# Who ends an upsampling kernel: GpSimd releases the other engines before the last store has landed, and ends alone

## The chip, the cores and the metric

One core of a Trainium2 chip. The metric is the device time of one execution in microseconds, the median of several; every run is of one core, with a granted clock of 1.0. "Span" is the time from the first to the last instruction of the program itself in a profiled execution; it is shorter than the measured time, and this case is about why.

In the profile, POOL is GpSimd, DVE is VectorE, ACT is ScalarE, PE and PEld are TensorE, and SP is SyncE, which issues the transfers; a "q" behind the name marks an instruction that the engine's sequencer (the part that runs its instruction stream) handles alone. Three such instructions make up the program's closing block: an EVENT_SEMAPHORE waits for semaphores, changes one, or both; a RANGE_CLEAR sets a row of semaphores to zero; a DRAIN stands here between other instructions, and can wait for a semaphore too. "Landing" is the moment of the last store's final semaphore increment.

## The reference

Nearest-neighbour upsampling by 2: each pixel of 16 x 64 images of 64 x 64 floats is written four times.

```python
batch, channels, h, w = (16, 64, 64, 64)
...
for i in range(new_h):
    for j in range(new_w):
        src_i = i // scale_factor
        src_j = j // scale_factor
        result[:, :, i, j] = x[:, :, src_i, src_j].copy()
```

That is 16.78 MB in and 67.11 MB out.

## The kernel before

SP issues five loads and twelve stores; VectorE and ScalarE expand the rows in between. The stores are 4 MB or 8 MB, and the last one is 8 MB:

```python
nc.vector.tensor_copy(out=u[:, :kv], in_=expanded(xp[:, r0 : r0 + kv, :]))
nc.scalar.copy(out=u[:, kv:], in_=expanded(xp[:, r0 + kv : r0 + k, :]))
...
return nc.sync.dma_start(out=dst[:, r0 : r0 + k, :], in_=u)
```

Two hooks rearrange the finished program. One issues the first load before the opening barrier. The other, which is what changes, rearranges the closing block. That block has GpSimd gather all engines and release them, twice; between the two it must wait for all stores and set the semaphores back to zero for the next execution. The kernel before already had GpSimd wait for the stores (a cut of its lines):

```python
d0, gather0, release0, d1, clear, d2, gather1, release1 = mine
landed = mybir.InstDrain(          # waits for all ten semaphores, the last store's too
    name=wait.name, engine=pool, ...
    sync_info=mybir.SyncInfo(on_wait=waits, on_update=[]),
)
others = [i for i in end if i.engine != pool and i is not wait]
blocks[-1].instructions = others + [
    d0, gather0, release0, gather1, d1, landed, clear, d2, release1
]
```

`clear` zeroes the ten semaphores 99 to 108; 99 is the one that the last store raises (and the first load and an earlier store: 3 x 16 = 48). `release1` lets the other four engines end.

## Time and profile before

| | kernel before |
|---|---|
| median of the first three runs | 199.01 us (198.98 to 199.02) |
| span of the profiled run | 197.41 us |
| its measured time | 199.19 us |
| last packet of the last store ends | 196.70 us |
| semaphore 99 complete (the landing) | 197.037 us |
| GpSimd's last instruction ends | 197.326 us |
| last instruction of the program (TensorE) ends | 197.414 us |
| last record of the runtime's barrier, semaphore 2 | 199.319 us |

The lines behind the upper half are in the prediction below. The last row is not on the profile's page; it comes from the trace's records of semaphore updates, which go on after the program. Here they are, for the kernel before, in ns after the landing:

```
semaphore 2:   +612 +646 +851 +895 +919  +1017 +1056 +1090 +1137
resets:        207..255 from +1036, 156.. from +1154, 54.. from +1195, the lowest block ends at +1700
semaphore 2:   +1925 +1959 +1997 +2041 +2065  +2163 +2201 +2235 +2282
```

The nine updates are one pass of a barrier over five engines, which sign it in turn: five updates going up and four coming back. The measured time is 0.13 us less than the time of the very last update (199.19 against 199.319 here).

### The profile page before, as it was taken

Reading aid. Unit: us, or ns where it says so; the run is one execution under the profiler, and the core shown is the slowest. Engines: PE = TensorE matmul, PEld = TensorE weight load, DVE = VectorE, ACT = ScalarE, POOL = GpSimd, SP = SyncE. Lnnn points to the kernel's source line nnn. Section 1 sums busy time; section 2 is a strip of 40 time slices with the busy share of each in tenths; the row PEclk is TensorE's granted clock in tenths of the full one; section 3 lists DMA queues with packets and bytes.
Section 4 is the critical chain, followed back from the end, with each engine's and each line's share of the span. In section 5 each row is a group of like instructions: output and inputs, shape, how many; then the busy total and the mean of one; then the engine's idle time right before and its main releaser. Section 6 shows DMA issues by size and latency. Waiting matters only on the chain.

```text
span 197.4 us, 117 instructions
## 1 busy us (share of the span) xinstructions
DVE 40.2 (20%) x12; ACT 51.3 (26%) x13; POOL 0.2 (0%) x4
## 2 busy tenths in 40 slices
DVE  0045000000505059505050007200810091000000
ACT  2047000000505060606079107400840093000000
POOL 0000000000000000000000000000000000000000
DMA  8999999999999999999999999999999999999994
GB/s 319 425 425 425 438 445 418 411 452 451 432 425 438 425 432 432 425 432 425 425 425 425 425 425 425 478 505 438 438 438 438 438 438 425 425 425 425 425 425 212
DMA packets 2448, 83.89 MB, mean 425 GB/s; under 512 B 272, under 2 KB 272, under 8 KB 400
## 3 DMA queue, kind: packets, MB, share of 16 engines
q1 hardware_dynamic: 2448, 83.89, 98.9%
HBM read 16.78 MB, written 67.11 MB: 425 GB/s over the span
## 4 chain that ended last, share of the span: by engine, by line
DMA 71%; ACT 11%; SPq 1%; issue 0%; ACTq 0%
DMA out_dram<-mem 52%; DMA mem<-in_x_dram 19%; ACT mem L140 11%; SPq L124 0%; SPq L142 0%; ACTq L140 0%
## 5 line engine op out<-in xcount | busy, mean ns | idle before, releaser
L140 ACT COPY mem<-mem 128x3584 f32<-128x3584 f32 (+1 forms) x12 | 50.0, 4174 | 112.5 <-DMA out_dram<-mem 102.1
L139 DVE COPY mem<-mem 128x4608 f32<-128x4608 f32 (+1 forms) x12 | 40.2, 3360 | 123.1 <-DMA out_dram<-mem 110.6
L140 ACT ACT_TABLE_LOAD x1 | 1.3, 1283 | 0.8 <-PEq L178 0.8
L178 POOL MEMSET const-bfloat16-1.0<- 128x1 bf16 x1 | 0.1, 102 | 0.0
L178 POOL MEMSET const-uint8-127<- 128x1 uint8 x1 | 0.1, 101 | 0.0
L178 POOL MEMSET const-float32-0.0<- 128x1 f32 x1 | 0.1, 99 | 0.2 <-issue 0.2
L178 POOL MEMSET const-float32-1.0<- 128x1 f32 x1 | 0.1, 98 | 0.0
## 6 DMA issues: line engine op xcount, KB each, us to landing
out_dram<-mem SPq DMA_DIRECT2D x8, 4096.0 KB, 16.2
mem<-in_x_dram SPq DMA_DIRECT2D x3, 4096.0 KB, 21.4
mem<-in_x_dram SPq DMA_DIRECT2D x1, 3328.0 KB, 38.1
mem<-in_x_dram SPq DMA_DIRECT2D x1, 768.0 KB, 39.4
out_dram<-mem SPq DMA_DIRECT2D x4, 32.4
```

Source lines behind the costliest of these rows:

```text
L139: nc.vector.tensor_copy(out=u[:, :kv], in_=expanded(xp[:, r0 : r0 + kv, :]))
L140: nc.scalar.copy(out=u[:, kv:], in_=expanded(xp[:, r0 + kv : r0 + k, :]))
L178: nc = _bacc.Bacc("TRN2", target_bir_lowering=False, num_devices=1)
```

## The change

The intent is to have as little as possible left to do once the last store has landed. GpSimd releases the others before it waits, clears nine semaphores after the second-last store, and sets the tenth back by the same instruction that waits for it.

```diff
@@
-    waits = sorted(wait.sync_info.on_wait, key=lambda w: w.id != last)
+    waits = list(wait.sync_info.on_wait)
...
+    lo, hi = clear.ant_dict["range_first"], clear.ant_dict["range_last"]
+    clears = []
+    for a, b in ((lo, last), (last + 1, hi + 1)):
+        if a < b:
+            clears.append(nc.gpsimd.sem_clear(range(a, b)).ins)
     landed = mybir.InstDrain(
...
-        sync_info=mybir.SyncInfo(on_wait=waits, on_update=[]),
+        sync_info=mybir.SyncInfo(
+            on_wait=[w for w in waits if w.id != last], on_update=[]
+        ),
     )
+    (w,) = [w for w in waits if w.id == last]
+    final = mybir.InstEventSemaphore(
+        name=clear.name,
+        engine=pool,
...
+            on_wait=[w],
+            on_update=[
+                mybir.SyncUpdate(
...
+                    update_mode="sem-sub-imm",
+                    update_value=w.wait_value,
+                )
+            ],
...
     blocks[-1].instructions = others + [
-        d0, gather0, release0, gather1, d1, landed, clear, d2, release1
+        d0, gather0, release0, gather1, release1, d1, landed, *clears, d2, final
     ]
```

In the built program the range below 99 is empty, so there is one range clear, 100 to 108.

More of the change, by code (lines that the diff above doesn't have):

```diff
@@ L51, in close_on_gpsimd @@
     assert wait.engine == sp and isinstance(wait, mybir.InstDrain)
-    waits = sorted(wait.sync_info.on_wait, key=lambda w: w.id != last)
-    assert waits[0].id == last and len(waits) > 2
+    waits = list(wait.sync_info.on_wait)
+    assert len({w.id for w in waits}) == len(waits) > 2
+    assert all(w.wait_mode == "sem-ge-imm" for w in waits)
     mine = [i for i in end if i.engine == pool]
@@ L67, in close_on_gpsimd @@
     d0, gather0, release0, d1, clear, d2, gather1, release1 = mine
+    lo, hi = clear.ant_dict["range_first"], clear.ant_dict["range_last"]
+    assert lo <= last <= hi and all(lo <= w.id <= hi for w in waits)
+    clears = []
+    for a, b in ((lo, last), (last + 1, hi + 1)):
+        if a < b:
+            clears.append(nc.gpsimd.sem_clear(range(a, b)).ins)
     landed = mybir.InstDrain(
@@ L71, in close_on_gpsimd @@
         debug=wait.debug,
-        sync_info=mybir.SyncInfo(on_wait=waits, on_update=[]),
+        sync_info=mybir.SyncInfo(
[6 more added lines that the diff above has]
+        engine=pool,
+        debug=wait.debug,
+        sync_info=mybir.SyncInfo(
+            on_wait=[w],
+            on_update=[
+                mybir.SyncUpdate(
+                    sync_type=w.sync_type,
+                    id=w.id,
+                    ant_name=w.ant_name,
+                    update_mode="sem-sub-imm",
+                    update_value=w.wait_value,
+                )
+            ],
+        ),
     )
```

## The prediction

> **What bounds the kernel now.** I read the page first (its DMA rows and its chain), then the waits of the store queue, then the instructions of the program's closing block, and last the trace's own records of semaphore updates, because the change lies wholly in that closing block. The page says what the kernel is:
>
> ```profile
> span 197.4 us, 117 instructions
> ...
> DVE 40.2 (20%) x12; ACT 51.3 (26%) x13; POOL 0.2 (0%) x4
> ...
> DMA  8999999999999999999999999999999999999994
> GB/s 319 425 425 425 438 445 418 411 452 451 432 425 438 425 432 432 425 432 425 425 425 425 425 425 425 478 505 438 438 438 438 438 438 425 425 425 425 425 425 212
> ...
> q1 hardware_dynamic: 2448, 83.89, 98.9%
> ...
> DMA 71%; ACT 11%; SPq 1%; issue 0%; ACTq 0%
> ```
>
> The reader is to see that the DMA engines are busy from the first slice to the last: 83.89 MB at 425 GB/s is 197.4 us, the whole span. VectorE and ScalarE are busy a quarter of the time or less. Only the last slice is thin (212 GB/s, digit 4), so that is where a change of the ending can act. A table of stretches narrows it; its columns are the stretch, its length, busy time of VectorE, ScalarE and GpSimd, granted clock, DMA share and GB/s:
>
> ```profile
> 165.50:196.00 30.50, 0.00 (x0) 0.00 (x0) 0.00 (x0) 1.00 0.95 413
> 196.00:196.70 0.70, 0.00 (x0) 0.00 (x0) 0.00 (x0) 1.00 0.01 0
> 196.70:197.40 0.70, 0.00 (x0) 0.00 (x0) 0.00 (x0) 1.00 0.00 0
> ```
>
> After 196.70 us no byte moves. What fills the last 0.7 us is the closing block, listed by engine's queue (count, min/median/max ns, first and last start):
>
> ```profile
> L192 POOLq DRAIN  x2: 34/34/34, 197.1 to 197.2; - x2
> L192 POOLq EVENT_SEMAPHORE_RANGE_CLEAR  x1: 92/92/92, 197.1 to 197.1; - x1
> L192 POOLq EVENT_SEMAPHORE  x1: 17/17/17, 197.3 to 197.3; - x1
> L192 SPq EVENT_SEMAPHORE  x1: 17/17/17, 197.4 to 197.4; - x1
> L192 ACTq EVENT_SEMAPHORE  x1: 17/17/17, 197.4 to 197.4; - x1
> L192 DVEq EVENT_SEMAPHORE  x1: 21/21/21, 197.4 to 197.4; - x1
> L192 PEldq EVENT_SEMAPHORE  x1: 51/51/51, 197.4 to 197.4; - x1
> ```
>
> Line 192 is the end of the program. GpSimd waits for the last store (DRAIN), clears the ten semaphores 99 to 108 with one range clear, drains again, and raises the release semaphore; only then do SP, ScalarE, VectorE and TensorE pass their last wait. With the records to the nanosecond: the last store's final increment of semaphore 99 comes at 197.037; DRAIN 197.061 (34 ns); range clear 197.124 (92 ns); DRAIN 197.246 (34 ns); release 197.309 (17 ns); the four engines' last waits at 197.351, 197.356, 197.362 and 197.363, the last (TensorE, 51 ns) ending at 197.414, which is the span.
>
> The measured time is 199.01 us, 1.6 us more than the span, so something after the program counts too. The semaphore records go on past the span: semaphore 2 is raised nine times at 197.649, .683, .888, .932, .956, 198.054, .093, .127, .174; then semaphores 3 to 255 are written in five blocks of 49 to 51 (207 up from 198.073, 156 up from 198.191, 105 up from 198.228, 54 up from 198.232, the low ones last, to 198.737); then semaphore 2 again nine times, 198.962 to 199.319.
>
> **What the Trainium skill says.** "Runtime: NRT & Kernel Launch", section "Semaphores 0–2 are reserved", has 2 as the sync barrier; its section "The ~15µs preamble/postamble breakdown" puts after the kernel a barrier over all engines, a reset of 51 semaphores by each engine, and another barrier, and calls the barrier a serpentine over five engines of 44 ns a hop, 8 hops. The trace agrees: nine updates, most hops 24 to 47 ns, then the five blocks. "Perfetto Trace Analysis", section "Per-engine timelines" (HWDGE), says that the last descriptor writes the semaphore only after the earlier write is confirmed. The trace shows the last packet ending at 196.70 and the last increment at 197.04, 0.34 us that no ordering of the closing block can shorten. Its summary of sequencer-only instructions says the reported start is the moment the wait is satisfied; 197.037 to 197.061 gives 24 ns for that step here, and 177.690 to 177.713, 23 ns, for an event-semaphore wait on GpSimd.
>
> **The change part by part.** Loads, copies, stores and their waits are untouched: the comparison of the two programs' instruction orders shows the same rows with shifted line numbers on every engine. So all moves after 197.04 us.
>
> Moved early: the second gather and the release. In the kernel before, GpSimd already has everyone's gather at 165.462; now it releases at once, so the four other engines end near 165.6 us instead of 197.4. They then sit in the runtime's barrier for over 31 us, which costs nothing.
>
> Moved early too: the clear. Semaphore 99 is the lowest of the ten, so the range below it is empty and the built program has one range clear, 100 to 108. It runs once the second-last store has landed, that is after 177.71 us, together with d2: 92 and 34 ns, 19 us ahead of the last landing. The waits are nine instead of ten before it, and one instruction of waits is saved there as well, all hidden.
>
> Added at the end: one event-semaphore instruction that waits for 48 on semaphore 99 and subtracts 48. By the 23 ns from increment to start and 17 ns for such an instruction (43 with two waits) it starts at 197.060 and ends at about 197.08.
>
> Sum on GpSimd: it left its program at 197.309 + 0.017 = 197.326; now at 197.078. That is 0.248 us less. The four removed starts spell the same: 63 + 122 + 63 ns from DRAIN to release. On the span as the profile defines it, the last instruction was TensorE's at 197.414, so the span should fall by more, 0.336 us, to 197.08, all else equal.
>
> What of this reaches the measured time depends on who holds up the runtime's barrier. I read its order from the blocks that follow: the low block begins 0.217 us after the ninth update, the 54 block 0.105 after the eighth, 105 after the seventh, 156 after the sixth, and 207 0.117 after the fifth. That is the order TensorE, ScalarE, GpSimd, VectorE, SP, if the blocks are dealt in that order; the same barrier before the program (with its ninth update at -0.002) fits, for SP, first to leave it, issues the first instruction at 0.000. There the third update comes 38 ns after the second; at the end of the program it comes 205 ns after. So the third engine, GpSimd by this reading, is the late one: it needs 197.888 - 197.326 = 0.562 us from its last instruction to its update, whereas TensorE needs 0.235. After that third update everything runs on at fixed hops, 1.431 us to the last update. If GpSimd's 0.562 us stays, its update comes at 197.078 + 0.562 = 197.640 and the whole tail shifts by 0.248 us. The predicted time is 199.01 - 0.25 = 198.76 us, 0.12% less.
>
> **The rivals.** (1) The late third engine is not GpSimd, and its 0.5 us run from the release. Then with all others long waiting, GpSimd would reach the barrier as fast as TensorE does (0.235), its update would come at 197.31, and the gain would be up to 0.57 us: 198.4. Against it: the block order above. (2) The early ends move the barrier's cost elsewhere: GpSimd's 0.562 us may contain a fetch of the code that follows the program, or the subtraction may need more than 17 ns before it can go on. A new 0.1 to 0.2 us would leave 198.9. Against it: GpSimd passed two such wait-and-subtract instructions at 165.135 and 165.462 with 17 ns each, and the next started 78 and 81 ns later. (3) Nothing at all: the four engines, sent into the runtime's code at 165.6 us, fetch or poll while the store queue works, and disturb it; or the measured time is closed by something that does not follow GpSimd. Then 199.0, or a little above. Polling is not seen to hurt: at 165.9 to 196.7 GpSimd's waits stood beside 413 GB/s already. (4) A hang or wrong result if a semaphore were left non-zero: 99 rises to 48 in three transfers of 16 and is taken to 0, and the runtime's block reset includes it anyway.
>
> **The range and the chances.** The spread of the three runs is 0.04 us, so a quarter of a microsecond should be seen, but a different chip or another draw of the last stores' landing can move the whole by 0.1 us or so. Rival 1 draws the low end to 198.5, rivals 2 and 3 the high end to 199.0. Two per cent is 4 us, sixteen times the whole mechanism; and no more than about 0.9 us lies between the last landing and the third update. Faster by over 2% has 0.5%, slower by over 2% (only by disturbance or a slow draw) 0.5%, within 2% 99%.
>
> **What would show it.** Right: GpSimd's last instruction is one event-semaphore of 17 ns or so within 30 ns of the last increment of semaphore 99; the range clear stands near 177.9 us; the other engines' last instructions are near 165.6; the span is about 0.34 us shorter and the measured time only about 0.25; the third barrier update stays 0.56 us behind GpSimd's end, with the first two already made near 165.9. Wrong: a third update that follows GpSimd's end by 0.2 us (rival 1) or by 0.7 (rival 2), or a last landing that has itself moved by more than 0.1 us (rival 3), which would mean that the DMA stream and not the ending decided the difference.

## The result, and the profile after

| | before | changed |
|---|---|---|
| median, 6 runs each | 198.96 us (198.88 to 199.02) | 198.72 us (198.60 to 198.83) |
| ratio, with 95% interval | | 0.9988 (0.9976 to 1.0001) |
| span of the profiled run | 197.414 us | 196.840 us |
| landing | 197.037 us | 196.800 us |
| landing to the last barrier update | 2.282 us | 2.035 us |

Ratios here and below are the mean time of one kernel's fast runs over the mean of the other's of the same rounds, so not quite the ratio of the medians beside them. The medians differ by 0.24 us, and the interval just reaches 1. The timing alone does not establish the difference; the profiles, and the runs below, do.

The page of the changed kernel has the same DMA-filled span:

```profile
span 196.8 us, 117 instructions
...
DMA  8999999999999999999999999999999999999994
...
q1 hardware_dynamic: 2448, 83.89, 99.3%
```

Its closing block, by engine's queue (count, min/median/max ns, first and last start in us). First four of the ten lines of the stretch from 164.9 to 165.6 us:

```profile
L223 SPq EVENT_SEMAPHORE  x2: 17/17/17, 165.0 to 165.3; - x2
L223 ACTq EVENT_SEMAPHORE  x2: 17/17/17, 165.0 to 165.3; - x2
L223 DVEq EVENT_SEMAPHORE  x2: 21/21/21, 165.0 to 165.4; - x2
L223 PEldq EVENT_SEMAPHORE  x2: 51/51/51, 165.0 to 165.4; - x2
```

then the early clear, which has its own line of the source:

```profile
L77 POOLq EVENT_SEMAPHORE_RANGE_CLEAR  x1: 92/92/92, 177.7 to 177.7; - x1
```

and everything that the program still does after 196.5 us:

```profile
L223 POOLq EVENT_SEMAPHORE  x1: 17/17/17, 196.8 to 196.8; - x1
```

The reader is to see that both releases are over at 165.4 us, that the clear lies 19 us ahead of the end, and that of the eight instructions that closed the kernel before (two DRAINs, a range clear, five event-semaphores) a single one is left, of 17 ns. In ns after the landing, the semaphore records of the changed kernel read:

```
semaphore 2:   -31161 -31127  +602 +646 +669  +766 +806 +841 +887
semaphore 2:   +1677 +1711 +1750 +1794 +1817  +1916 +1954 +1988 +2035
```

Two of the five engines now sign the barrier 31 us early. The third, and with it all the rest, is 0.25 us earlier after the landing than before.

The profiled runs differ by more, 199.19 against 198.71. That is 0.247 us from the ending and 0.237 us from an earlier landing, which the change cannot have made: the first store was issued at 39.617 us against 39.864, before any instruction that differs, and from the last store's issue to its landing it took 32.440 us before and 32.444 after. Where a profile's start-to-end times are compared in quarters of a microsecond, they must be anchored at the landing; so I do for all runs.

### The profile page after: what moved, and what is told of

Read it like the earlier page. It is cut to its first block, busy times and chain, and to the rows that moved or that the text cites. A ratio compares the mean times of both kernels' runs of the same rounds, so it can differ in the third digit from the quotient of the medians.

```text
span 196.8 us, 117 instructions
## 1 busy us (share of the span) xinstructions
DVE 40.2 (20%) x12; ACT 51.3 (26%) x13; POOL 0.2 (0%) x4
## 4 chain that ended last, share of the span: by engine, by line
DMA 71%; ACT 11%; SPq 1%; issue 0%; ACTq 0%
DMA out_dram<-mem 52%; DMA mem<-in_x_dram 19%; ACT mem L171 11%; SPq L155 0%; SPq L173 0%; ACTq L171 0%
```

## The experiments

The theory: the time ends with GpSimd, which after its last instruction needs about 0.56 us to sign the runtime's barrier as the third of five; all after that is fixed. The rivals: the gain comes from the other four engines' early end; GpSimd's 0.56 us is itself only a wait for something else; or the difference was chance, a landing that happened to come early. Nine runs were made, seven edits and two repeats; all were correct, all in the fast state, and by the rule of 2% all are "same" as the kernel before. In all of them the last store took 32.43 to 32.46 us from issue to landing.

| kernel | engine that the barrier waits for: its end after the landing (in brackets an engine that ended later) | its barrier update (place) | landing to last update | median us | ratio to before (95%) |
|---|---|---|---|---|---|
| before | GpSimd 0.289 (TensorE 0.377) | 0.851 (3rd) | 2.282 | | 1 |
| changed | GpSimd 0.040 | 0.602 (3rd) | 2.035 | 198.72 | 0.9988 (0.9976 to 1.0001) |
| early release alone | GpSimd 0.243 | 0.768 (3rd) | 2.199 | 198.89 | 0.9996 (0.9983 to 1.0010) |
| early clear alone | GpSimd 0.119 (TensorE 0.206) | 0.680 (3rd) | 2.111 | 198.80 | 0.9992 (0.9979 to 1.0004) |
| changed, 8 DRAINs more | GpSimd 0.565 | 1.089 (3rd) | 2.522 | 199.11 | 1.0007 (0.9995 to 1.0020) |
| SP ends alone | SP 0.033 | 0.167 (5th) | 1.476 | 198.14 | 0.9962 (0.9949 to 0.9974) |
| TensorE ends alone | TensorE 0.080 | 0.359 (1st) | 1.862 | 198.62 | 0.9978 (0.9963 to 0.9993) |
| VectorE ends alone | VectorE 0.049 | 0.232 (4th) | 1.618 | 198.40 | 0.9966 (0.9949 to 0.9982) |
| ScalarE ends alone | ScalarE 0.038 | 0.178 (2nd) | 1.647 | 198.27 | 0.9961 (0.9946 to 0.9975) |
| changed, again | GpSimd 0.041 | 0.602 (3rd) | 2.033 | 198.72 | 0.9988 (0.9975 to 1.0002) |
| SP ends alone, again | SP 0.033 | 0.167 (5th) | 1.476 | 198.18 | 0.9960 (0.9948 to 0.9973) |

The first four experiments shared a chip (kernel before there 198.99 us, 9 runs), the next three another call (199.03 us, 7 runs), the last two a third (198.97 us, 9 runs).

**Early release alone.** The kernel before, with one instruction moved:

```diff
-        d0, gather0, release0, gather1, d1, landed, clear, d2, release1
+        d0, gather0, release0, gather1, release1, d1, landed, clear, d2
```

> Kernel before with one part of the change: GpSimd releases the other engines early (about 165.3 us), but still does its wait for the last store, the range clear of all ten semaphores and a DRAIN at the end. Theory (the time ends with GpSimd: its last instruction, then 0.56 us to its update of the runtime's barrier, then 1.43 us of fixed hops and resets): only the release instruction leaves the end of GpSimd's program, 63 ns of start spacing less its 17 ns in place of the DRAIN's 34, so 0.046 us; from last landing to last barrier update 2.236 us (before 2.282), time about 198.91 against 198.96. Rival (the gain comes from the other four engines having ended early, not from GpSimd): the whole gain, 2.035 us from landing to last update, 198.72.

Its program from 190 us on:

```profile
L192 POOLq DRAIN  x2: 34/34/34, 196.9 to 197.1; - x2
L192 POOLq EVENT_SEMAPHORE_RANGE_CLEAR  x1: 92/92/92, 196.9 to 196.9; - x1
```

Measured 2.199 us, 198.89 us. The four engines are done as early as in the changed kernel (their last instructions end 31.4 us before the landing), yet only 0.083 of the 0.247 us is gained. The rival is out: the early end of the others is worth nothing by itself. The theory's 2.236 missed by 0.037 us. GpSimd ended where expected, 0.243 us after the landing, but its update followed after 0.525 us, not 0.562. The difference has a counterpart inside the program: on GpSimd the next instruction starts 60 to 64 ns after the start of a DRAIN of 34 ns, and 78 to 81 after that of an event-semaphore of 17 that changes a semaphore (where it is not held up by a wait), that is 26 to 30 ns and 61 to 64 ns after their ends. Ending on a DRAIN hands over some 37 ns sooner.

**Early clear alone.** The changed kernel, with the release put last:

```diff
-        d0, gather0, release0, gather1, release1, d1, landed, *clears, d2, final
+        d0, gather0, release0, gather1, d1, landed, *clears, d2, final, release1
```

> Changed kernel with the other part alone: the clear is early and the last wait subtracts, but the release of the other engines comes after it, as GpSimd's last instruction. Theory: GpSimd ends one event-semaphore (78 ns start to start) later than in the changed kernel, 0.12 us after the landing, and the other engines, ending 0.1 us after that, still reach the barrier before it; landing to last update 2.035 + 0.078 = 2.11 us, time about 198.79, third update still 0.56 us after GpSimd's end. Rival (other engines' early end is the gain): 2.28 us, 198.96.

```profile
L223 POOLq EVENT_SEMAPHORE  x2: 17/17/17, 196.7 to 196.7; - x2
L223 SPq EVENT_SEMAPHORE  x1: 17/17/17, 196.8 to 196.8; - x1
L223 ACTq EVENT_SEMAPHORE  x1: 17/17/17, 196.8 to 196.8; - x1
L223 DVEq EVENT_SEMAPHORE  x1: 21/21/21, 196.8 to 196.8; - x1
L223 PEldq EVENT_SEMAPHORE  x1: 51/51/51, 196.8 to 196.8; - x1
```

That is all after 196.5 us. Measured 2.111 us, as expected, and 198.80 us. The four engines end last again, TensorE 0.087 us after GpSimd, and it makes no difference: TensorE's update comes at 0.441, ScalarE's at 0.475, and then the pass waits until 0.680 for GpSimd's, 0.561 us after its end.

**Eight DRAINs more.** The changed kernel with a dose on GpSimd behind its last wait:

```diff
-        d0, gather0, release0, gather1, release1, d1, landed, *clears, d2, final
+        d0, gather0, release0, gather1, release1, d1, landed, *clears, d2, final,
+        *[mybir.InstDrain(name=f"I-{90001 + k}", engine=pool, debug=wait.debug) for k in range(8)],
```

> Changed kernel with eight DRAINs added on GpSimd after the last wait, a known length on the engine said to be late. Theory: GpSimd's end moves by 81 + 7 x 63 + 34 - 17 = 0.54 us, all of it reaches the time: landing to last update 2.57 us, time 199.26. Rival (GpSimd is not the late engine; something fixed runs from the landing, and GpSimd's 0.56 us is waiting for it): the first half of the drains is hidden, 198.7 to 199.0, and the 0.56 us from its end to the third update shrinks.

```profile
L224 POOLq DRAIN  x8: 34/34/34, 196.8 to 197.2; - x8
L224 POOLq EVENT_SEMAPHORE  x1: 17/17/17, 196.7 to 196.7; - x1
```

GpSimd's end moved from 0.040 to 0.565 us after the landing, its update from 0.602 to 1.089, the last update from 2.035 to 2.522. Nothing was hidden: 0.487 us from update to update and 0.487 us at the end. That GpSimd's half microsecond is only a wait for another engine is out, for then the first drains would have cost nothing. It is 0.05 us less than expected, for the two reasons just seen: DRAINs follow each other at 61 ns, not 63, and after a DRAIN the update comes after 0.524 us. The median, 199.11 us, is 0.12 above the kernel before of these rounds where the records give 0.24; the timing's scatter is of that size, and its interval holds both.

**SP ends alone.** The same last instruction on another engine:

```diff
     final = mybir.InstEventSemaphore(
         name=clear.name,
-        engine=pool,
+        engine=mybir.EngineType.SP,
 ...
-        d0, gather0, release0, gather1, release1, d1, landed, *clears, d2, final
-    ]
+        d0, gather0, release0, gather1, release1, d1, landed, *clears, d2
+    ] + [final]
```

> Changed kernel with the last wait and subtraction on SP and not on GpSimd; GpSimd ends after its early clear. Theory (serpentine order TensorE, ScalarE, GpSimd, VectorE, SP read from the reset blocks; GpSimd slow to the barrier): four updates of semaphore 2 are made long before, SP makes the fifth within about 0.24 us of its end (TensorE's figure, an estimate for SP), then 1.36 us to the last: landing to last update 0.03 + 0.24 + 1.36 = 1.63 us against 2.035, time about 198.3, faster than both kernels. Rival (any engine that ends last costs the same 0.56 us and a full serpentine): 198.7. Rival 2 (block order does not give the serpentine order): more than one update left after SP's end in the first pass, and 198.5 or more.

After 190 us the program has one instruction:

```profile
L223 SPq EVENT_SEMAPHORE  x1: 17/17/17, 196.8 to 196.8; - x1
```

and the records are, in ns after the landing:

```
semaphore 2:   -31159 -31125 -18483 -18439  +167  +211 +249 +283 +331
semaphore 2:   +1120 +1154 +1192 +1236 +1259  +1357 +1396 +1430 +1476
```

This confirms the reading of the order: with SP last exactly four updates are made early, the third (GpSimd's) once GpSimd has done its clear at about 19 us before the landing. Measured 1.476 us and 198.14 us, 0.56 us less than the changed kernel after the landing. It is faster than the kernel before with an interval clear of 1. When both ran again on one chip (below) all five of its times, 198.05 to 198.43 us, lay under all five of the changed kernel's, 198.62 to 199.01. The expected 1.63 us was 0.15 too long. SP took 0.134 us from its end to its update, not TensorE's 0.24. And the step back from the fifth to the sixth update took 44 ns, where it takes 97 to 99 in every other kernel; why it is shorter when SP is the late one, the records do not say.

**TensorE, VectorE, ScalarE end alone.** The same edit with `PE`, `DVE` and `Activation`:

> As the run with SP ending alone, with the last wait and subtraction on TensorE. Theory (the place in the serpentine and the engine's own time to the barrier set the cost): TensorE's instruction ends 0.07 us after the landing (51 ns long), its update follows 0.235 us later and is the first of the nine, then hops of 34, 38, 44 and 23 ns to the fifth, then 1.31 to 1.37 us: 1.75 to 1.81 us from landing to last update, time about 198.45; no update of semaphore 2 before the landing. Rival (the order is not TensorE, ScalarE, GpSimd, VectorE, SP): some updates already made before the landing.

> The same with VectorE ending alone. Theory: ends 0.037 us after the landing, its update is the fourth (three made long before), 0.13 to 0.24 us after its end (between SP's and TensorE's figures), 23 ns to the fifth, then 1.31 to 1.37 us: 1.50 to 1.66 us, time about 198.25. Rival: a slow engine like GpSimd with 0.5 us to the barrier: 1.9 us, 198.6; or another number of updates left.

> The same with ScalarE ending alone. Theory: ends 0.033 us after the landing, its update is the second (one made before), 0.13 to 0.24 us later, then 38, 44 and 23 ns to the fifth and 1.31 to 1.37 us: 1.58 to 1.75 us, time about 198.35. Rival: as for VectorE, 0.5 us to the barrier and 198.65, or another number of updates left.

The last instruction of the program, in these three kernels in turn:

```profile
L223 PEldq EVENT_SEMAPHORE  x1: 51/51/51, 197.0 to 197.0; - x1
```

```profile
L223 DVEq EVENT_SEMAPHORE  x1: 21/21/21, 196.9 to 196.9; - x1
```

```profile
L223 ACTq EVENT_SEMAPHORE  x1: 17/17/17, 196.8 to 196.8; - x1
```

The number of updates made before the landing was zero, three and one, so with SP's four and GpSimd's two the order TensorE, ScalarE, GpSimd, VectorE, SP is now shown, not only read from the blocks. VectorE (1.618 us) and ScalarE (1.647) fell inside what was expected. TensorE (1.862) came 0.05 us above: its update followed 0.279 us after its end, where it was 0.235 in the kernel before, and its wait ended 29 ns after the landing, not 16. The first difference is not explained. The medians of VectorE and ScalarE stand the other way round than their records, by 0.13 us; landings alone differ by 0.075 us between their two profiles, and I take the records for the order.

**Both again, on one chip.**

> The changed kernel again, unaltered, because the interval of its first runs reached 1. Theory: from landing to last barrier update 2.035 us again, to 5 ns; time 0.25 us below the kernel before of the same chip, ratio about 0.9988. Rival (the first difference was a draw of the stores' landing): a ratio nearer to 1.000, with the landing-to-last figure unchanged or not.

> SP ending alone again, beside the changed kernel on one chip. Theory: 1.476 us from landing to last update, to 5 ns, so 0.56 us below the changed kernel and 0.81 below the one before, ratio to before about 0.9960. Rival (the earlier run drew early landings): the ratio rises towards 0.998.

2.033 and 1.476 us, ratios 0.9988 and 0.9960. The changed kernel gave the same ratio twice, from different executions; each interval by itself just includes 1, while the figure from landing to last update repeats to 2 ns. None of the edits touches a store before its landing, and the landing still lay anywhere between 196.638 and 196.936 us over the nine runs; that scatter blurs the timings.

## Why the prediction was right

It said 198.76 us and 198.72 was measured, 0.24 us below the kernel before, where the working gave 0.248. That the medians agree to a hundredth of a microsecond is partly luck, since the six single runs span 0.14 us for the kernel before and 0.23 us for the changed one; the agreement that counts is that of the records after the landing, term by term:

- *GpSimd's end moves by 0.248 us.* Shown: 0.289 to 0.040 after the landing, 0.249.
- *The late engine of the barrier is GpSimd, 0.562 us from its last instruction to its update.* Shown: 0.562 in both kernels, 0.561 in the early clear alone, and the dose of DRAINs passed through whole. Where SP or VectorE ends last, GpSimd signs 19 us before the landing with the first two updates long made, and still needs 0.524 and 0.525 us after its DRAIN: it is not a wait for another engine's update. What fills that half microsecond stays open; it is in the runtime's part, of which the records show only the updates. The prediction's thought of a fetch of code finds no support: the trace's DMA records name packets of a queue "instruction", but in all eleven profiles the last of them starts no later than 0.07 us after the first instruction. None stands near GpSimd's early end, where the records still run.
- *Everything after the third update is fixed, 1.431 us.* Shown: 1.431 to 1.433 us from the third update to the last in the five different kernels in which GpSimd's is the late one.
- *The span falls by 0.336 us.* Of the profiled spans' 0.574 us, 0.337 is the ending (0.377 to 0.040 after the landing) and 0.237 the landing.
- *Rival 1 (up to 0.57 us) and rival 2 (0.1 to 0.2 us lost)* did not happen. *Rival 3*, disturbance of the stores, is not seen: the last store's 32.44 us did not change. Its test in the prediction, a landing moved by more than 0.1 us, was badly chosen: the landing moved by 0.24 us because the loads before happened to end earlier. The test should have been the time from the last issue to the landing.
- The prediction placed the marks of the changed kernel by the old trace: the others' last instructions near 165.6 (seen 165.4), the first two updates near 165.9 (165.64 and 165.67), the clear near 177.9 (177.66). The shift of the stores, 0.25 us at the first one's issue, accounts for most of it.
- *Four of its readings are loose, though none enters the sum.* The DMA rows and the table of stretches count a whole packet where it starts. The last sixteen packets of 64 KB start at 193.6 to 194.3 us and run until 196.05 to 196.69. By the packet records the DMA engines were busy for 76% of the last slice, not 4 tenths, and for 35% of 196.0 to 196.7 us, where the table has 0.01 and 0 GB/s. So the thin last slice is largely a matter of counting; what shows the room at the end is that the last packet ends at 196.70. The closing block does not fill the last 0.7 us either, but only what follows 197.06; before it, 0.34 us pass until the landing. ScalarE's 26% is a little over a quarter. And the lowest block of resets shows 46 updates, of semaphores from 7 to 53, not 49 from 3 up.

The two parts of the change do not share the gain evenly. From the kernel before to the early release alone is 0.083 us, to the early clear alone 0.171, together 0.247, so they add within 7 ns. About 0.037 us of the first is due to what instruction GpSimd ends with.

What the prediction did not ask is whether GpSimd should end last at all. By its own figures TensorE needs 0.235 us to the barrier and GpSimd 0.562, so it could have seen that another engine would do better; moving one instruction to SP gains another 0.56 us, over twice what the whole change gained.

## What to carry to other kernels

When a kernel ends on a transfer, what counts is what lies between the last increment of its semaphore and the runtime's barrier: leave one instruction there, and clear and release before it. Put that instruction on the engine that is quickest to the barrier and late in its order; here that is SP, not GpSimd. Judge such quarters of a microsecond from the last landing onward, since the landing itself moves by as much from run to run. The order and the times are those of this program on one core, under the runtime of these runs.

## What the Trainium skill lacked or had wrong

- "Runtime: NRT & Kernel Launch", "The ~15µs preamble/postamble breakdown", puts 1.5 us for the barrier after the kernel, 1.5 us for the semaphore reset and 2 us for the second barrier with the rearming of rings. Here the whole tail, from the program's end to the last update, is 1.905 us in the kernel before: the resets 0.66 us (1.036 to 1.700 after the landing), the second pass 0.357 us; a rearming of rings leaves no mark in these records, and one after the last update would not show. Its 44 ns a hop and 8 hops, about 355 ns, fit that second pass as a sum; single hops there are 24 to 98 ns.
- The same section gives the serpentine without an order. These runs show TensorE, ScalarE, GpSimd, VectorE, SP, and back.
- No page read for this has the time from an engine's last instruction to its barrier update: SP 0.134 us, ScalarE 0.140, VectorE 0.183, TensorE 0.235 and 0.279, GpSimd 0.524 to 0.562.
- "Perfetto Trace Analysis", "Per-engine timelines", calls the waiting and the semaphore's propagation that a profile leaves out of a sequencer-only instruction its hidden tail, and gives no figure for what lies between one such instruction and the next. On GpSimd the start of the next comes 60 to 64 ns after the start of a DRAIN shown as 34 ns, and 78 to 81 ns after that of an event-semaphore shown as 17 ns that changes a semaphore.
- The same section says that the semaphore write behind a store to HBM can be surprisingly late, without a figure there (another page of the skill has rough figures for the completion of a transfer). The last store's final increment came 0.34 us after its last packet's end (196.70 to 197.04 us) in the kernel before, and 0.32 to 0.36 us in all eleven profiles. That last packet, of 4 bytes, ends 5 or 6 ns after the last one of data.
